# RMSNorm statistics of a two-layer trunk: the squares summed to one tile on GpSimd, the statistics placed behind the first group of products

## Chip, cores and metric

The kernel runs on one core of a Trainium2 chip. The metric is the device time of one execution in microseconds (us), the median of three runs. The core's engines are named as in the profile: PE (TensorE matmuls), DVE (VectorE), ACT (ScalarE), POOL (GpSimd), SP (SyncE, which issues most DMAs).

## What is computed

The reference is a trunk of two layers over 256 tokens of width 1024, in float32:

```python
for i in range(DEPTH):                       # DEPTH = 2
    h = h + 0.5 * swiglu(rmsnorm(h, ffn1_norm[i]), ffn1_w_up[i], ffn1_w_down[i])
    h = h + token_mixer(rmsnorm(h, mix_norm[i]), ...)   # FoX | retention | SSD | HGRN2, one W_in, one W_out
    h = h + 0.5 * swiglu(rmsnorm(h, ffn2_norm[i]), ffn2_w_up[i], ffn2_w_down[i])
    gate = sigmoid(rmsnorm(h, ple_norm[i]) @ ple_w_gate[i])
    h = h + gate * (p[i] @ ple_w_proj[i])
return rmsnorm(h, final_norm)

def rmsnorm(x, w):
    return x * lax.rsqrt(jnp.mean(x * x, axis=-1, keepdims=True) + 1e-6) * w
```

There are eight norms ahead of products (four in each layer) and a last one on the output.

## The kernel before

The state H lies transposed in SBUF: 128 partitions hold 128 of the 1024 channels, and `H[:, d]` (d = 0 to 7) is one such slice over 256 tokens. Every product is computed from float32 operands that are split in a high and a low part. `weight` brings 512 KB of a matrix to a buffer `raw`; L166 casts it on ACT to the high part `wh`, L167 subtracts on DVE for the low part `wl`. Some 360 such weights, one behind the other, are the stream that PE lives on.

**A norm.** `Norm.part` (L189) forms slice d of the normalised input without its row factor: `y` is H times the gain, high part on ACT (L194), low part on DVE (L195). The row factor 1/rms is applied to the products, afterwards. So the first products can start when the first slices of H are there, and the statistics follow: `square` (L203) squares two slices at a time on ACT (L205, 128x512); GpSimd adds the squares of slices 0 to 5 (L207, two adds of 128x512) and folds the sum to 128x256 (L210); slices 6 and 7 stay a tile of their own. `stats` (L212) sums over partitions on PE: `mm2` (L112) multiplies a 128x128 block by a column of ones in two matmuls of 64 output rows; one block of the folded tile and two of the last tile for either half of the tokens make 12 matmuls, which are 24 records in the trace. `rsqrt` (L233) makes the factors out of the two columns by nine small DVE operations (L237 to L246). `spread` (L225) copies them over the partitions by two transposing matmuls (`rows`, L106), and ACT copies that to the tile `rb` (L229), which every later scaling reads.

**Where that stands.** `col_group` (L261) and `col_tiles` emit the first group of products of a norm: four units (ffn) or two column tiles (mixer, gate) in an order in which each slice of the norm is used as it comes. `xn.scale()` (stats and rsqrt) stands at step 24 of 32 of that group, `xn.spread()` at its end. In `ffn` (L335) the group's four units are the first two of 22 gate/up pairs; `product` (L348) then adds the two halves of a bank, multiplies by the row factor (L358), applies SiLU and splits the result. Each later pair f takes two `unit`s and one `product`. In the down phase each of eight output slices is scaled, added to H, and is the next norm's part. In `mixer` the group gives hf and hq, the inputs of HGRN2 (`scaled`, L432); then come two token tiles `hv` of 264 columns (L294 to L296, in one bank of pool p and one of m), which hold also the eight small columns of dt and the forget gate (`small`, lines from L720), and after these the list PROJ. HGRN2 begins with a sigmoid and a logarithm (L571 to L577, a table load on ACT among them), a scan (L599), differences (L638 to L650), the scores (L674, L679 on PE, `qt` from L666) and masks (L690), and gives its output at L706. The last norm of layer 1 is inside `ending`, whose own call of `scale` is between products.

**What sets the order.** The program text is one order; a list scheduler decides for each engine which ready instruction is issued next, by priorities that follow the program text, and each engine runs its own list strictly in order. So text that moves lets other instructions move too. PSUM banks come from pools p (2), m (2) and a (4); squares from a pool of seven tiles m2; weights from 4 `raw`, 8 `wh` and 8 `wl`.

Of the kernel before, what the change touches and what calls it, by code (L numbers as in the profile page):

```python
# [14 lines left out]
AF = mybir.ActivationFunctionType  # L15
# [4 lines left out]
P = 128  # L20
S = 256
# [13 lines left out]
AHEAD = 2  # L35
START = "x0 u00 u10 x1 u20 u30 u01 x2 u11 u21 x3 u31"
LAG = 6
SCALE_AT = 24
ORDER = (3, 2, 1, 0)
PROJ = ("fv", "bc", "rq", "xs", "fk", "rk", "hg", "fq", "sz", "rg")  # L40

# [23 lines left out]
def trunk(ctx, tc, x, pt, par_d, con_d, w_d, ws_d, fin_d, out):  # L65
# [18 lines left out]
    def tw(kind, dt=F32, width=1024):  # L84
        if kind in ("raw", "wh", "wl"):
            return T([P, WIDE], kind, dt, NB[kind])[:, 0:width]
        return T([P, 512], kind, dt, NB[kind])
# [10 lines left out]
    def v2(t):  # L98
        return t.rearrange("p (a b) -> p a b", a=2)

    def flat(t):
        return t.rearrange("p a b -> p (a b)")
# [5 lines left out]
    def mm2(o, lhsT, rhs, start, stop):  # L108

        for u in range(2):  # L110
            r = slice(64 * u, 64 * u + 64)
            mm(o[r], lhsT[:, r], rhs, start=start, stop=stop, skip_group_check=True)  # L112
# [71 lines left out]

    class Norm:
        def __init__(self):
            self.x, self.h, self.l, self.sq = [], [], [], []

        def part(self, d, l, name, first=False):  # L189
            if d % 2 == 0:  # L190
                self.y = pair()
            y = self.y[:, d % 2]
            w = prm(l, name, d)
            A.mul(y[:, 0], H[:, d], w)  # L194
            V.scalar_tensor_tensor(y[:, 1], H[:, d], w, y[:, 0].bitcast(F32),  # L195
                                   ALU.mult, ALU.subtract)
            self.x.append(flat(y))
            self.h.append(y[:, 0])
            self.l.append(y[:, 1])
            if d % 2 and not first:  # L200
                self.square(d // 2)

        def square(self, c):  # L203
            sq = tw("m2")
            A.activation(sq, flat(H[:, 2 * c:2 * c + 2]), AF.Square)  # L205
            if self.sq and c < 3:
                G.tensor_add(sq, sq, self.sq.pop())  # L207
            self.sq.append(sq)
            if c == 2:
                G.tensor_add(sq[:, 0:S], sq[:, 0:S], sq[:, S:])  # L210

        def stats(self):  # L212
            self.b = bank("a")
            n = len(self.sq)
            for c, sq in enumerate(self.sq):
                for d in range(1 if c == 0 else 2):
                    for t in range(2):
                        mm2(self.b[:, t:t + 1], v2(sq)[:, d, t * P:(t + 1) * P], ones1,
                            c == 0 and d == 0 and t == 0, c == n - 1 and d == 1)

        def scale(self):
            self.stats()
# [38 lines left out]
    def col_group(units, xn, one, terms, arrival=None, lag=0):  # L261

        rank = arrival or (lambda u, k: k // 2)
        order = sorted((rank(u, k), u, k) for u in range(len(units)) for k in range(KD))
        for n in range(len(order) + lag):
            if n == len(order) * SCALE_AT // 32:
                xn.scale()
            if n < len(order):
                one(units[order[n][1]], order[n][2], terms[0])
            if n >= lag:  # L270
                one(units[order[n - lag][1]], order[n - lag][2], terms[1])
        xn.spread()

    def col_tiles(targets, xn, k_outer=False):
        def one(unit, k, terms=(0, 1, 2)):
# [59 lines left out]
    def ffn(xn, l, name, after_first=None, arrival=None, lag=0):  # L335
# [9 lines left out]
        def one(unit, k, terms=(0, 1)):  # L345
            b, (wh, wl) = unit
            prod2(b, wh[:, k], wl[:, k], xn.x[k], k == 0, k == KD - 1, terms)
# [19 lines left out]

        units = [unit() for _ in range(4)]
        col_group(units, xn, one, ((0,), (1,)), arrival, lag)
        for f in range(2):  # L370
            product(units[2 * f][0], units[2 * f + 1][0])
        for f in range(2, NF // P):
            units = [unit(), unit()]
            for u in units:
                for k in range(KD):
                    one(u, k)
            if f == 7 and after_first is not None:
                after_first()
            product(units[0][0], units[1][0])
# [45 lines left out]
    def mixer(l, xn):  # L425
# [26 lines left out]
        def projections():  # L452
            ba, bb = bank("p"), bank("p")
            wa, wb = by_column(), by_column()
            col_tiles(((ba, wa), (bb, wb)), xn, k_outer=True)
            got["hf"] = scaled(ba, o=v2(tw("h2")))
            got["hq"] = scaled(bb, o=keep("hq"))
            yield
            hv = keep("hv")
            bh = [bank("p"), bank("m")]  # L460
            for n, w in enumerate(by_row(2, HIW)):
                token_tiles([b[:, 0:HIW] for b in bh], w, xn, 4 * n, (n == 0, n == 0), n == 1)
                yield
            for t in range(2):
                A.mul(hv[:, t], bh[t][:, 0:256], xn.col[:, t:t + 1])
            got["hv"] = hv
# [596 lines left out]
            begin[n](int(st[2]))  # L1063
    A.dma_start(con[:, :128], con_d[:, :128])
    A.dma_start(par[1], par_d[1])
    for c in range(4):
        xn.square(c)

    def arrival(u, k):
        return max(steps.index(f"x{k // 2}"), steps.index(f"u{u}{k // 4}"))  # L1070
# [1 line left out]
    for l in range(DEPTH):  # L1072
# [13 lines left out]
        for c in range(4):  # L1086
# [5 lines left out]
                         ph[:, k], pl[:, k], m == 0 and k == 0, k == 1)  # L1092
            bp.append(b)

        def gate(c):
            w = by_column()
            z = tw("m2")
            b = bank("a")
            col_tiles(((b, w),), xn, k_outer=(c == 0))
            V.tensor_mul(v2(z), v2(b), xn.rb)  # L1100
            A.activation(z, z, AF.Sigmoid)
            V.tensor_mul(z, z, bp[c])  # L1102
            V.tensor_add(hpair(c), hpair(c), z)
# [117 lines left out]
```

## Time and profile before

| | us |
|---|---|
| median of three runs | 1112.73 |
| lowest and highest | 1109.96 and 1114.6 |
| profiled execution, its own time | 1111.85 |
| span in that profile | 1110.1 |

The profile is one execution of the program. The span is what lies between its first and last instruction; 1.75 us of the execution lie around it. Its mean granted clock of PE is 0.996. Of the page the first part gives each engine's busy time, the fourth the chain of work that ended last, followed back from the end. "Idle before" is how long an engine stood still ahead of an instruction, with an arrow to what released it. Matmuls are pipelined, so neighbours in a list overlap: what one costs is read from the distance of starts.

### The profile page before, as it was taken

What the parts mean: (1) busy time and instruction counts of PE and PEld (TensorE: products, weight loads), DVE (VectorE), ACT (ScalarE), POOL (GpSimd) and SP (SyncE); (2) the same over time, 40 slices, a digit from 0 to 9 for tenths busy, and PEclk for the clock granted to TensorE, in tenths of its full rate; (3) what the DMA queues carried; (4) which work ended last, traced back from release to release, by engine and by line L of the source; (5) the groups of instructions that cost most, each with busy time, mean ns of one, the idle gap of its engine ahead of it and who ended that gap; (6) DMA issues with size and microseconds to landing.
All of it is one profiled execution on the core that took longest, in us unless ns stands there. A gap on an engine that the chain in (4) does not pass through costs nothing.

```text
span 1110.1 us, 18572 instructions
## 1 busy us (share of the span) xinstructions
PE 1080.3 (97%) x7178; PEld 960.0 (86%) x7178; DVE 839.0 (76%) x1454; ACT 638.8 (58%) x1063; POOL 39.9 (4%) x40
## 2 busy tenths in 40 slices
PE   7999999999999999999999999999999999999996
PEld 5888888889897888888988888898899888888885
DVE  6887767599779777767878777757997787777655
ACT  6665545445477555544668555545446765555443
POOL 2000001000001000000000000001000100000001
PEclk9999999999999999999999999999999999999998
DMA  8776556135356655555555666651444476655541
GB/s 261 263 252 188 187 188 190 58 118 186 117 170 200 218 190 188 185 182 188 181 168 176 210 189 187 188 172 54 130 141 153 139 256 194 189 188 185 187 134 38
DMA packets 55432, 193.96 MB, mean 175 GB/s; under 512 B 6576, under 2 KB 7088, under 8 KB 55344
## 3 DMA queue, kind: packets, MB, share of 16 engines
q1 hardware_dynamic: 54192, 191.06, 53.8%
q10 hardware_dynamic: 1152, 1.72, 0.5%
q8 instruction: 56, 0.92, 0.3%
q14 instruction: 32, 0.26, 0.1%
HBM read 190.66 MB, written 1.05 MB: 173 GB/s over the span
## 4 chain that ended last, share of the span: by engine, by line
PE 84%; DVE 9%; ACT 3%; DMA 3%; issue 2%; SPq 0%; ACTq 0%; DVEq 0%
PE bank_a L257 27%; PE bank_a L259 14%; PE bank_p L251 10%; PE bank_m L257 8%; PE bank_p L257 8%; PE bank_m L259 4%; PE bank_p L259 4%; PE bank_a L251 3%; DVE wl L167 2%; DMA raw<-w 2%; DVE wl L690 1%; ACT wh L166 1%; DVE qt L666 1%; PE bank_a L112 1%; DVE y L195 1%
## 5 line engine op out<-in xcount | busy, mean ns | idle before, releaser
L167 DVE TENSOR_TENSOR wl<-raw,wh 128x1024 fp32r<-128x1024 f32 (+2 forms) x360 | 438.0, 1223 | 174.7 <-ACT wh L166 174.0
L166 ACT CAST wh<-raw 128x1024 fp32r<-128x1024 f32 (+2 forms) x360 | 371.7, 1040 | 328.6 <-issue 194.3
L257 PE MATMUL bank_a<-y,wh 128*128 128x512 f32 x576 | 203.0, 394 | 0.0
L259 PE MATMUL bank_a<-y,wl 128*128 128x256 f32 x576 | 161.8, 281 | 0.0
L257 PE MATMUL bank_p<-y,wh 128*128 128x512 f32 x416 | 150.6, 399 | 7.8 <-DVE y L195 7.8
L257 PE MATMUL bank_m<-y,wh 128*128 128x512 f32 x416 | 150.3, 397 | 0.2 <-DVE m L1102 0.2
L251 PE MATMUL bank_p<-y,wh 128*128 128x256 f32 x720 | 135.8, 287 | 0.0
L257 PEld LDWEIGHTS bank_a<-y,wh 128*128 128x128 f32 x576 | 108.1, 188 | 25.0
L259 PE MATMUL bank_m<-y,wl 128*128 128x256 f32 x416 | 116.1, 281 | 5.0 <-DVE wl L167 5.0
L259 PE MATMUL bank_p<-y,wl 128*128 128x256 f32 x416 | 117.1, 282 | 0.0
L251 PEld LDWEIGHTS bank_p<-y,wh 128*128 128x128 f32 x720 | 111.5, 189 | 2.7 <-issue 1.7
L259 PEld LDWEIGHTS bank_a<-y,wl 128*128 128x128 f32 x576 | 108.5, 188 | 0.0
L251 PE MATMUL bank_p<-y,wl 128*128 128x256 f32 x360 | 102.3, 284 | 0.9 <-DVE wl L167 0.9
L257 PEld LDWEIGHTS bank_p<-y,wh 128*128 128x128 f32 x416 | 78.5, 189 | 26.7 <-ACT wh L166 6.6
L257 PEld LDWEIGHTS bank_m<-y,wh 128*128 128x128 f32 x416 | 78.6, 189 | 18.6 <-issue 0.5
L259 PEld LDWEIGHTS bank_m<-y,wl 128*128 128x128 f32 x416 | 78.3, 189 | 5.8 <-DVE wl L167 5.6
L259 PEld LDWEIGHTS bank_p<-y,wl 128*128 128x128 f32 x416 | 78.6, 189 | 0.2
L251 PE MATMUL bank_a<-y,wh 128*128 128x256 f32 x384 | 71.8, 285 | 0.0
L251 PEld LDWEIGHTS bank_p<-y,wl 128*128 128x128 f32 x360 | 68.1, 189 | 1.5 <-DVE wl L167 1.0
L251 PEld LDWEIGHTS bank_a<-y,wh 128*128 128x128 f32 x384 | 59.6, 189 | 0.4 <-issue 0.3
L207 POOL TENSOR_TENSOR m<-m,m 128x512 f32<-128x512 f32 x16 | 22.0, 1374 | 959.5 <-ACT m L205 664.9
L251 PE MATMUL bank_a<-y,wl 128*128 128x256 f32 x192 | 54.0, 284 | 0.0
(419 smaller groups left out, 1897.1 us busy)
## 6 DMA issues: line engine op xcount, KB each, us to landing
raw<-w SPq DMA_DIRECT2D x348, 512.0 KB, 4.1
raw<-ws SPq DMA_DIRECT2D x4, 528.0 KB, 4.5
raw<-w SPq DMA_DIRECT2D x8, 256.0 KB, 5.1
con<-con SPq DMA_DIRECT2D x3, 512.0 KB, 7.4
H<-x SPq DMA_DIRECT2D x4, 256.0 KB, 5.8
m<-rk SPq DMA_DIRECT2D x8, 64.0 KB, 4.0
m<-rq SPq DMA_DIRECT2D x8, 64.0 KB, 2.2
m<-pt ACTq DMA_DIRECT2D x2, 256.0 KB, 3.4
```

What stands on the lines that cost most here:

```text
L112: mm(o[r], lhsT[:, r], rhs, start=start, stop=stop, skip_group_check=True)
L166: A.copy(h[:, cs], r[:, cs])
L167: last_dve[0] = V.tensor_sub(lo[:, cs], r[:, cs], h[:, cs].bitcast(F32)).ins
L195: V.scalar_tensor_tensor(y[:, 1], H[:, d], w, y[:, 0].bitcast(F32), ALU.mult, ALU.subtract)
L207: G.tensor_add(sq, sq, self.sq.pop())
L251: mm(o, wl if n == 2 else wh, xl if n == 1 else xh, start=first and n == 0, stop=last and n == 2, skip_group_check=True)
L257: mm(b, wh, x, start=first, stop=False, skip_group_check=True)
L259: mm(b[:, S:], wl, x[:, 0:S], start=False, stop=last, skip_group_check=True)
L666: V.tensor_mul(o, q0, e0)
L690: V.copy_predicated(pf[r].rearrange("p (h c n two e) -> p c h n two e", h=8, c=2, two=2, e=L)[:, u, :, :, 1], K("lvl", m, m + 32)[r].rearr ...
```

## The change

1. **Squares.** `square` is called for each slice. Slices 0 to 5 go in pairs as before, with the fold behind them. Then slice 6 and slice 7 are each squared alone (128x256) into the free half of the sum's tile and added on GpSimd (128x256). Each of the two squares has to wait for GpSimd's operation before it, which still reads that half.
2. **Statistics.** `stats` has one tile left: 4 matmuls instead of 12, so 8 records in a trace instead of 24.
3. **Place.** `col_group` calls neither `scale` nor `spread`. In `ffn` the next pair, f = 2, is emitted first: `scale` behind its first unit, `spread` behind its second, and the two products of the group after that. In `mixer` the two token tiles hv come directly behind the group, in two banks of pool m, with `scale` and `spread` behind the first and the second half; hf and hq are scaled after that. In the gate of layer 0 the products of the second slice pair are put between `scale` and `spread`. The place in `ending` stays.

```diff
--- before.py
+++ after.py
@@ -35,7 +35,6 @@
 AHEAD = 2
 START = "x0 u00 u10 x1 u20 u30 u01 x2 u11 u21 x3 u31"
 LAG = 6
-SCALE_AT = 24
 ORDER = (3, 2, 1, 0)
 PROJ = ("fv", "bc", "rq", "xs", "fk", "rk", "hg", "fq", "sz", "rg")
 
@@ -184,7 +183,7 @@
 
     class Norm:
         def __init__(self):
-            self.x, self.h, self.l, self.sq = [], [], [], []
+            self.x, self.h, self.l = [], [], []
 
         def part(self, d, l, name, first=False):
             if d % 2 == 0:
@@ -197,26 +196,29 @@
             self.x.append(flat(y))
             self.h.append(y[:, 0])
             self.l.append(y[:, 1])
-            if d % 2 and not first:
-                self.square(d // 2)
-
-        def square(self, c):
-            sq = tw("m2")
-            A.activation(sq, flat(H[:, 2 * c:2 * c + 2]), AF.Square)
-            if self.sq and c < 3:
-                G.tensor_add(sq, sq, self.sq.pop())
-            self.sq.append(sq)
-            if c == 2:
-                G.tensor_add(sq[:, 0:S], sq[:, 0:S], sq[:, S:])
+            if not first:
+                self.square(d)
+
+        def square(self, d):
+
+            if d < 6:
+                if d % 2:
+                    sq = tw("m2")
+                    A.activation(sq, flat(H[:, d - 1:d + 1]), AF.Square)
+                    if d > 1:
+                        G.tensor_add(sq, sq, self.sq)
+                    self.sq = sq
+                if d == 5:
+                    G.tensor_add(sq[:, 0:S], sq[:, 0:S], sq[:, S:])
+                return
+            sq = self.sq
+            A.activation(sq[:, S:], H[:, d], AF.Square)
+            G.tensor_add(sq[:, 0:S], sq[:, 0:S], sq[:, S:])
 
         def stats(self):
             self.b = bank("a")
-            n = len(self.sq)
-            for c, sq in enumerate(self.sq):
-                for d in range(1 if c == 0 else 2):
-                    for t in range(2):
-                        mm2(self.b[:, t:t + 1], v2(sq)[:, d, t * P:(t + 1) * P], ones1,
-                            c == 0 and d == 0 and t == 0, c == n - 1 and d == 1)
+            for t in range(2):
+                mm2(self.b[:, t:t + 1], self.sq[:, t * P:(t + 1) * P], ones1, t == 0, True)
 
         def scale(self):
             self.stats()
@@ -263,13 +265,10 @@
         rank = arrival or (lambda u, k: k // 2)
         order = sorted((rank(u, k), u, k) for u in range(len(units)) for k in range(KD))
         for n in range(len(order) + lag):
-            if n == len(order) * SCALE_AT // 32:
-                xn.scale()
             if n < len(order):
                 one(units[order[n][1]], order[n][2], terms[0])
             if n >= lag:
                 one(units[order[n - lag][1]], order[n - lag][2], terms[1])
-        xn.spread()
 
     def col_tiles(targets, xn, k_outer=False):
         def one(unit, k, terms=(0, 1, 2)):
@@ -367,13 +366,17 @@
 
         units = [unit() for _ in range(4)]
         col_group(units, xn, one, ((0,), (1,)), arrival, lag)
-        for f in range(2):
-            product(units[2 * f][0], units[2 * f + 1][0])
+        first = [(units[2 * f][0], units[2 * f + 1][0]) for f in range(2)]
         for f in range(2, NF // P):
             units = [unit(), unit()]
-            for u in units:
+            for n, u in enumerate(units):
                 for k in range(KD):
                     one(u, k)
+                if f == 2:
+                    (xn.scale, xn.spread)[n]()
+            if f == 2:
+                for pair_of in first:
+                    product(*pair_of)
             if f == 7 and after_first is not None:
                 after_first()
             product(units[0][0], units[1][0])
@@ -453,14 +456,14 @@
             ba, bb = bank("p"), bank("p")
             wa, wb = by_column(), by_column()
             col_tiles(((ba, wa), (bb, wb)), xn, k_outer=True)
+            hv = keep("hv")
+            bh = [bank("m"), bank("m")]
+            for n, w in enumerate(by_row(2, HIW)):
+                token_tiles([b[:, 0:HIW] for b in bh], w, xn, 4 * n, (n == 0, n == 0), n == 1)
+                (xn.scale, xn.spread)[n]()
             got["hf"] = scaled(ba, o=v2(tw("h2")))
             got["hq"] = scaled(bb, o=keep("hq"))
             yield
-            hv = keep("hv")
-            bh = [bank("p"), bank("m")]
-            for n, w in enumerate(by_row(2, HIW)):
-                token_tiles([b[:, 0:HIW] for b in bh], w, xn, 4 * n, (n == 0, n == 0), n == 1)
-                yield
             for t in range(2):
                 A.mul(hv[:, t], bh[t][:, 0:256], xn.col[:, t:t + 1])
             got["hv"] = hv
@@ -1063,8 +1066,8 @@
             begin[n](int(st[2]))
     A.dma_start(con[:, :128], con_d[:, :128])
     A.dma_start(par[1], par_d[1])
-    for c in range(4):
-        xn.square(c)
+    for d in range(KD):
+        xn.square(d)
 
     def arrival(u, k):
         return max(steps.index(f"x{k // 2}"), steps.index(f"u{u}{k // 4}"))
@@ -1092,12 +1095,23 @@
                          ph[:, k], pl[:, k], m == 0 and k == 0, k == 1)
             bp.append(b)
 
+        banks = {}
+
+        def products(c):
+            banks[c] = bank("a")
+            w = by_column()
+            col_tiles(((banks[c], w),), xn, k_outer=(c == 0))
+
         def gate(c):
-            w = by_column()
+            if c == 0:
+                products(0)
+                xn.scale()
+                products(1)
+                xn.spread()
+            elif c > 1:
+                products(c)
             z = tw("m2")
-            b = bank("a")
-            col_tiles(((b, w),), xn, k_outer=(c == 0))
-            V.tensor_mul(v2(z), v2(b), xn.rb)
+            V.tensor_mul(v2(z), v2(banks[c]), xn.rb)
             A.activation(z, z, AF.Sigmoid)
             V.tensor_mul(z, z, bp[c])
             V.tensor_add(hpair(c), hpair(c), z)
```

In the new text the lines are numbered anew: L166 is the subtraction for `wl` (before L167), L111 the statistics' matmul (L112), L105 the transpose (L106), L239 to L248 the rsqrt (L237 to L246), L435 `scaled` (L432), L580 the start of HGRN2 on DVE (L577), L643 its third difference (L640).

What moves is shown at two places. The first is DVE in the first ffn of layer 0, around the factors of the first norm (rv, ry and rt are the three small tiles of rsqrt, wl a weight's low part, m a product's tile). Before:

```order
L238 TENSOR_SCALAR ry_33_227<-rv_32_226 128x2
L240 SCALAR_TENSOR_TENSOR rt_34_228<-ry_33_227 128x2
L167 TENSOR_TENSOR wl_167<-raw_165,wh_166 128x1024
L241 TENSOR_TENSOR rt_34_228<-rt_34_228,rv_32_226 128x2
L242 SCALAR_TENSOR_TENSOR rt_34_228<-rt_34_228 128x2
L243 SCALAR_TENSOR_TENSOR ry_33_227<-rt_34_228,ry_33_227 128x2
L167 TENSOR_TENSOR wl_289<-raw_287,wh_288 128x1024
L244 SCALAR_TENSOR_TENSOR rt_34_228<-ry_33_227 128x2
L357 TENSOR_TENSOR m_35_264<-m_35_264,bank_p_155 128x256
L245 TENSOR_TENSOR rt_34_228<-rt_34_228,rv_32_226 128x2
L361 TENSOR_TENSOR m_35_264<-m_35_264,bank_m_156 128x256
L246 SCALAR_TENSOR_TENSOR ry_33_227<-rt_34_228,ry_33_227 128x2
```

After:

```order
L166 TENSOR_TENSOR wl_340<-raw_338,wh_339 128x1024
L243 TENSOR_TENSOR rt_41_274<-rt_41_274,rv_39_272 128x2
L166 TENSOR_TENSOR wl_347<-raw_345,wh_346 128x1024
L244 SCALAR_TENSOR_TENSOR rt_41_274<-rt_41_274 128x2
L166 TENSOR_TENSOR wl_397<-raw_395,wh_396 128x1024
L245 SCALAR_TENSOR_TENSOR ry_40_273<-rt_41_274,ry_40_273 128x2
L360 TENSOR_TENSOR m_46_326<-m_46_326,bank_a_244 128x256
L246 SCALAR_TENSOR_TENSOR rt_41_274<-ry_40_273 128x2
L166 TENSOR_TENSOR wl_404<-raw_402,wh_403 128x1024
L247 TENSOR_TENSOR rt_41_274<-rt_41_274,rv_39_272 128x2
L356 TENSOR_TENSOR m_56_383<-m_56_383,bank_a_337 128x256
L248 SCALAR_TENSOR_TENSOR ry_40_273<-rt_41_274,ry_40_273 128x2
```

Before, two subtractions stand among the nine operations; after, four, and they are the ones of the weights that follow the pair f = 2.

The second place is DVE in the mixer of layer 0, where HGRN2 starts (h, lk, hb and kk are its tiles, sm and smo those of `small`, dc a sum from PE, cc a sum from PE that `small` leads to). Before:

```order
L432 TENSOR_TENSOR hq_2149<-bank_p_1997,rb_2145 128x512
L577 SCALAR_TENSOR_TENSOR h_348_2152<-h_346_2147,h_347_2151 128x512
L720 SCALAR_TENSOR_TENSOR sm_366_2274<-bank_p_2168,ry_344_2108,par_65 128x8
L578 TENSOR_TENSOR lk_2154<-h_348_2152,h_346_2147 128x512
L599 SCALAR_TENSOR_TENSOR hb_2162<-con,h_348_2152 128x512
L720 SCALAR_TENSOR_TENSOR sm_366_2274<-bank_m_2169,ry_344_2108,par_65 128x8
L601 TENSOR_TENSOR h_349_2164<-hq_2149,kk_2153 128x512
L603 TENSOR_TENSOR lk_2154<-lk_2154,hb_2162 128x512
L617 COPY dc_2215<-bank_a_2206 128x8
L638 COPY h_362_2220<-hb_2162 128x2x64
L639 TENSOR_TENSOR h_362_2220<-hb_2162 128x2x64
L640 TENSOR_TENSOR h_362_2220<-lk_2154,hb_2162 128x2x64
```

After:

```order
L857 COPY cc_2289<-bank_m_2284 128x8
L580 SCALAR_TENSOR_TENSOR h_354_2203<-h_352_2198,h_353_2202 128x512
L581 TENSOR_TENSOR lk_2205<-h_354_2203,h_352_2198 128x512
L602 SCALAR_TENSOR_TENSOR hb_2213<-con,h_354_2203 128x512
L604 TENSOR_TENSOR h_355_2215<-hq_2200,kk_2204 128x512
L606 TENSOR_TENSOR lk_2205<-lk_2205,hb_2213 128x512
L620 COPY dc_2263<-bank_a_2254 128x8
L641 COPY h_371_2268<-hb_2213 128x2x64
L642 TENSOR_TENSOR h_371_2268<-hb_2213 128x2x64
L643 TENSOR_TENSOR h_371_2268<-lk_2205,hb_2213 128x2x64
L644 TENSOR_TENSOR h_371_2268<-lk_2205,hb_2213 128x2x64
L166 TENSOR_TENSOR wl_2296<-raw_2294,wh_2295 128x1024
```

Before, HGRN2's first operation on DVE (L577) follows `scaled` directly and the chain of `small` comes after the differences; after, all of `small` up to its last copy (cc) stands ahead of HGRN2's first operation (L580), and a weight's subtraction (wl_2296) stands behind the differences.

## Rows read from the trace of the kernel before

**Rows 1.** The page: busy time of each engine, and the chain that ended last.

```profile
PE 1080.3 (97%) x7178; PEld 960.0 (86%) x7178; DVE 839.0 (76%) x1454; ACT 638.8 (58%) x1063; POOL 39.9 (4%) x40
...
PE 84%; DVE 9%; ACT 3%; DMA 3%; issue 2%; SPq 0%; ACTq 0%; DVEq 0%
```

**Rows 2.** Windows: stretch, length, busy PE, PEld, DVE, ACT, POOL, clock, DMA share, GB/s.

```profile
220.00:240.00 20.00, 18.47 (x161) 15.25 (x160) 19.11 (x55) 10.40 (x20) 0.84 (x1) 1.00 0.34 106
...
320.00:345.00 25.00, 22.25 (x166) 20.66 (x163) 21.86 (x25) 17.01 (x25) 3.42 (x3) 1.00 0.59 190
...
765.00:785.00 20.00, 17.86 (x141) 15.03 (x140) 17.93 (x52) 10.57 (x20) 0.58 (x1) 0.91 0.33 105
```

**Rows 3.** Chain of waits, mixer of layer 0: start, length, engine, tile, line, count.

```profile
197.00 8.59 PE bank_p L251 x72
205.58 0.80 PE bank_a L112 x24
```

**Rows 4.** Timeline of GpSimd, second ffn's norm of layer 0: start, length, instruction, idle before.

```profile
335.24 2.71 POOL L207 TENSOR_TENSOR m<-m,m 128x512 f32<-128x512 f32 x2 [114.40 <-DVE y L195]
338.03 0.79 POOL L210 TENSOR_TENSOR m<-m 128x256 f32<-128x256 f32 x1
```

**Rows 5.** Timeline of DVE, first norm of layer 0.

```profile
21.23 0.15 DVE L241 TENSOR_TENSOR rt<-rt,rv 128x2 f32<-128x2 f32 x1
21.42 0.16 DVE L242 SCALAR_TENSOR_TENSOR rt<-rt 128x2 f32<-128x2 f32 x1
...
21.70 1.23 DVE L167 TENSOR_TENSOR wl<-raw,wh 128x1024 fp32r<-128x1024 f32 x1
22.84 0.15 DVE L244 SCALAR_TENSOR_TENSOR rt<-ry 128x2 f32<-128x2 f32 x1
...
23.64 0.15 DVE L246 SCALAR_TENSOR_TENSOR ry<-rt,ry 128x2 f32<-128x2 f32 x1
```

**Rows 6.** Timeline of DVE, mixer of layer 0.

```profile
210.49 0.69 DVE L432 TENSOR_TENSOR h<-bank_p,rb 128x512 f32<-128x512 f32 x1 [2.33 <-ACT rb L229]
...
214.58 0.69 DVE L577 SCALAR_TENSOR_TENSOR h<-h,h 128x512 f32<-128x512 f32 x1 [2.80 <-ACT h L576]
...
219.01 1.98 DVE L640 TENSOR_TENSOR h<-lk,hb 128x128 f32<-128x128 f32 x1
```

**Rows 7.** Timeline of ACT, mixer of layer 0.

```profile
211.96 1.28 ACT L573 ACT_TABLE_LOAD   x1
```

**Rows 8.** Timeline of PE, mixer of layer 0.

```profile
222.64 2.15 PE L674 MATMUL bank_a<-qt,kt 128*128 128x128 f32 x16 [1.36 <-DVE qt L666]
...
249.89 0.40 PE L706 MATMUL bank_a<-wl,hv 128*64 128x128 f32 x2 [0.36 <-DVE wl L690]
```

**Rows 9.** Timeline of PE, mixer of layer 1.

```profile
772.45 3.74 PE L674 MATMUL bank_a<-qt,kt 128*128 128x128 f32 x16 [2.14 <-ACT wh L166]
...
797.54 0.40 PE L706 MATMUL bank_a<-wl,hv 128*64 128x128 f32 x2 [0.36 <-DVE wl L690]
```

**Rows 10.** Windows, mixer of layer 1.

```profile
770.00:775.00 5.00, 2.86 (x13) 2.36 (x12) 4.89 (x16) 2.79 (x6) 0.00 (x0) 0.74 0.01 2
775.00:780.00 5.00, 5.00 (x44) 4.26 (x43) 3.58 (x13) 3.23 (x6) 0.00 (x0) 0.92 0.68 210
```

**Rows 11.** Timeline of DVE, second ffn's norm of layer 0.

```profile
335.74 2.50 DVE L195 SCALAR_TENSOR_TENSOR y<-H,par,y 128x256 fp32r<-128x256 f32 x2
338.16 1.75 DVE L167 TENSOR_TENSOR wl<-raw,wh 128x1024 fp32r<-128x1024 f32 x1
339.83 0.87 DVE L195 SCALAR_TENSOR_TENSOR y<-H,par,y 128x256 fp32r<-128x256 f32 x2
```

**Rows 12.** Timeline of PE, second ffn's norm of layer 0.

```profile
339.96 0.39 PE L259 MATMUL bank_m<-y,wl 128*128 128x256 f32 x1 [2.75 <-DVE wl L167]
```

**Rows 13.** Timeline of ACT, the ending.

```profile
1087.53 1.28 ACT L1033 ACT_TABLE_LOAD   x1 [3.16 <-DVE ry L246]
```

**Rows 14.** Timeline of DVE, mixer of layer 1.

```profile
758.45 0.69 DVE L577 SCALAR_TENSOR_TENSOR h<-h,h 128x512 f32<-128x512 f32 x1 [2.80 <-ACT h L576]
```

## The prediction

> **What bounds the kernel now.** I read the page first. PE is busy 97% of the span and holds 84% of the chain that ended last; DVE, at 76%, holds 9% of it [rows 1]. So time goes only with matmuls taken from PE, and comes with every new PE idle. The second view is the windows by stage: outside the first and last 25 us, PE stands still in few places, and there DVE is near full. In the mixer of layer 0, DVE works 19.1 of 20 us while PE misses 1.5; at the second ffn's norm PE misses 2.75; in the mixer of layer 1, 2.1 [rows 2]. The change moves DVE work in all three. The third view is the chain around one norm: 72 matmuls of 256 columns take 8.59 us (0.119 each, so about 0.23 for 512 columns), and directly behind them the statistics take 0.80 us for 24 records, 33 ns a record, in the same row without a gap [rows 3]. They lie on the path.
>
> **What is removed.** 16 records less per norm at 33 ns: 0.53 us, eight times, 4.3 us in all. That is 0.39% of the time, under the 0.5% (5.6 us) that a measurement here can tell from no change. The Trainium skill ("TensorE: Matmul & The Clock Gate", section on LDWEIGHTS) gives a weight load a time that grows with its columns; for the 64 columns of these matmuls an estimate by it is 53 ns a record, 6.8 us in all and a forecast 2.5 us lower. The trace has a duration, 33 ns, and it decides.
>
> **What is added.** Per norm two GpSimd adds of 128x256. One such fold took 0.79 us [rows 4]; GpSimd is 4% busy, so 16 of them fit. But a square on ACT waits for each, and the operations behind that square in ACT's list (weight casts) wait with it. ACT is 58% busy; away from a norm's start this is covered.
>
> **What moves, norm by norm** (profiled execution, 1111.85 us; it lies 0.9 below the median, and the three runs spread over 4.7, so I leave the sum where it falls).
>
> *First norm.* The nine rsqrt operations start 0.195 us apart; before, two weight subtractions stand among them, 1.14 us each from start to start, and they end at 23.64 [rows 5]. After, the statistics run one unit later, at about 24.8, and four subtractions and four small adds stand among the nine: 4 x 1.14 + 9 x 0.195 + 4 x 0.34 = 7.7 us at least, 32.8, and some 33.9 if the subtractions' casts wait for their weights as before. PE reaches the transposes five eighths into the fourth unit behind the group (2.8 us each, ending the group at 22.0): 22.0 + 0.3 + 3.6 x 2.8 = 32.4. So PE waits 1.5 us, with 0 and 3 as the ends (casts never late; each later subtraction held up once). Net +1.0.
>
> *Mixer of layer 0.* Before, hf and hq are scaled at 210.49, and HGRN2 begins on DVE at 214.58 [rows 6], behind a table load of 1.28 us on ACT [rows 7]. After, two half token tiles (24 matmuls of 264 columns, 2.9 us each) come between group and transposes, so scaling starts about 5 us later, at 215.5; the 17 small operations of `small` and a second table load now stand ahead, and HGRN2 begins at some 220.7, 6.1 us later. PE meanwhile has more to do, as the hv tiles no longer stand behind: by counting matmuls in the two orders at the rates above, 48.1 us of PE work lie between the group's end and HGRN2's output instead of 45.4. But it idles in new places: 1.3 us where the FoX value tiles want the two banks of pool p that hf and hq still hold, 1.3 at the sum that waits for the scan, and 3.8 where a weight's subtraction stands behind the third difference, the operation that took 1.98 us beside GpSimd [rows 6]. DVE paces from there on. My walk ends with HGRN2's output at 255.0 instead of 249.89 [rows 8]: 5.1 later for 2.7 more done, +2.4; with the statistics, +1.9. The ends are 0 (the idles close up) and +6.1 (the delay passes on whole, nothing covered).
>
> *The clock.* An idle of 2.14 us in the mixer of layer 1 [rows 9] was followed by a granted clock of 0.74 and 0.92 in two stretches of 5 us, that is 3.4 us at the lower of the two levels (1.2 GHz) [rows 10]; the same 16 score matmuls took 3.74 us there and 2.15 in layer 0 [rows 8, 9], where PE had idled 1.36. That is a price of 1.6 us. The new idle of 3.8 in layer 0 is longer than the one that brought it, so I add 1.6; the ends are 0 and 3.2.
>
> *The two second ffns.* Here POOL's two adds run 335.24 to 337.95, and DVE's pair of `y` beside them takes 2.50 us against 0.87 two rows later [rows 4, 11]; the next subtraction is 1.75, and PE waits 2.75 us for it [rows 12]. Two more adds now follow in that place, and the third weight's cast waits for a square that waits for POOL. The cost of that is not in the trace: between nothing and one add, 0.79. I take 0.6, as DVE is the last wait here. Net +0.1, twice.
>
> *Gate of layer 0, first ffn of layer 1, ending.* In the first two, transposes come after a column tile or two units, by which rsqrt (1.75 us) is long done: -0.5 each. In the ending, PE's statistics lead straight through rsqrt to the table load that waits for it [rows 13]: -0.5.
>
> *Mixer of layer 1.* Same move as in layer 0: HGRN2 begins at 764.4 instead of 758.45 [rows 14], its output at 801.4 instead of 797.54 [rows 9], 3.9 later, for 51.4 us of PE work instead of 46.2. The idle is cut in many pieces of under 1.8 us, so the 1.6 us of lower clock go. Net -1.25, with the statistics -1.8; ends -3.4 and +2.
>
> **The sum.** +1.0 (first norm) +1.9 +1.6 (mixer 0, clock) +0.2 (two second ffns) -1.6 (gate, ffn, ending) -1.8 (mixer 1) = +1.3: 1113.1 us. The 4.3 us are saved and given back where DVE's list got longer ahead of something PE wants.
>
> **Rivals.**
>
> *B: the saving stays.* The list scheduler's new waits close up (a reorder absorbed by the deep list of weights that is ready), mixer 0 and the first norm lose nothing, and the lower clock of mixer 1 goes: -4.3 - 1.6, 1106.0. For it: PE is 97% busy and more of its work stands ahead of HGRN2. Against: DVE had 0.9 us free in 20 [rows 2], and its list there is in strict order.
>
> *C: slower, the mixers are paced by DVE.* Place: HGRN2's start, behind `small`. If both delays, 6.1 and 6.0, reach PE whole, because the matmuls that should cover them wait too (value tiles for banks, the rest for the subtraction behind the differences), the kernel gives 12.1 for 4.3: +7.8, 1119.7. It decides from 9.9 us lost in the two mixers (4.3 + 5.6). For it: DVE is full there [rows 2]. Against: in my walk half of the delay finds other matmuls.
>
> *D: GpSimd holds DVE.* The pair of `y` that took 2.50 us instead of 0.87 beside two adds [rows 4, 11] lost 1.63 us, 0.8 per add. If each of the two new adds in the first norm and the two second ffns holds DVE for its whole 0.79 us, and PE waits for DVE there, that is 6 x 0.79 = 4.7 us; 1.2 of it is in the sum, so 1116.6. The Trainium skill ("SBUF — State Buffer", section "SBUF: two separate sides") says that a VectorE operation with two SBUF inputs and a GpSimd operation that reads SBUF lock each other out of a shared port pair for a whole instruction; the trace agrees, with 2.50 against 0.87. Against D as a whole: by the time of the new adds most of DVE's `y` is done.
>
> *E: the change does less than it says.* The removed records could have been hidden; but the chain has them directly behind matmuls [rows 3], so I give this no chance of its own.
>
> **How the numbers follow.** My forecast (with its bounds) 0.56, B 0.18, C 0.16, D 0.10. Faster by over 0.5% means below 1107.2: most of B and the lowest edge of the forecast, 0.16. Slower means above 1118.3: nearly all of C, some of D and the forecast's upper edge, 0.21. Between, 0.63. The range goes from B's time to C's, 1106.0 to 1119.7, which leaves out some 0.1 on either side; the forecast's own ends (first norm, mixer 0 and clock at their bounds) lie within it.
>
> **What would show it.** Right: eight groups of 8 records in place of 24; PE idle of 1 to 2 us at the first norm's transposes; HGRN2 in layer 0 beginning 5 to 7 us later, a PE idle of 3 to 4 us some 4 us behind that, and the lower clock after it; no lower clock in the mixer of layer 1. Wrong: no new idle in mixer 0 (B), HGRN2's outputs 6 us late in both layers with no more PE work ahead of them (C), or `y` and subtractions at twice their length beside POOL in three norms, with PE waiting for them (D).

## The result: slower, and where the time went

The changed kernel takes 1124.2 us (median of 4 runs, 1123.09 to 1125.3) against 1112.97 of the kernel before in the same comparison: ratio 1.0108, with a 95% interval of 1.0082 to 1.0134. That is slower by 11.2 us by the medians (12.0 by the ratio), outside the range that was given (1106.0 to 1119.7), and on the side that had a chance of 0.21.

The page of the changed kernel, its first part, answers to [rows 1]:

```profile
PE 1083.3 (97%) x7050; PEld 959.0 (85%) x7050; DVE 846.0 (75%) x1454; ACT 642.1 (57%) x1071; POOL 52.6 (5%) x56
```

The 128 records of the statistics are gone (7178 to 7050). But the span grew from 1110.1 to 1121.7 us: PE stands idle 38.4 us instead of 29.8, and is busy 3.0 us longer although it has less to do. The second is the sign of a lower clock, and of waits whose restart the busy time swallows.

To see where, I cut both traces at the same events: the first or last DVE operation that writes H in each part. The differences in the table are worked out from the starts of those operations in the timelines; the ending goes from the last write of H to the end of ACT's last DMA issue.

| from one write of H to another | before, us | changed, us | change | forecast |
|---|---|---|---|---|
| start to the end of ffn 1, layer 0 | 200.09 | 200.19 | +0.1 | +1.0 |
| mixer, layer 0 | 135.05 | 141.64 | +6.6 | +3.5 |
| ffn 2, layer 0, to its first output slice | 135.68 | 137.74 | +2.1 | +0.1 |
| gate of layer 0 and ffn 1 of layer 1, to its first output slice | 161.18 | 163.87 | +2.7 | -1.1 |
| mixer, layer 1 | 137.55 | 137.86 | +0.3 | -1.8 |
| ffn 2, layer 1, to its first output slice | 135.90 | 136.25 | +0.4 | +0.1 |
| ending | 35.53 | 34.67 | -0.9 | -0.5 |

The three down phases between them took 0.4 us more together.

**The mixer of layer 0.** DVE's timeline of the changed kernel, at the place of [rows 6]:

```profile
215.69 0.69 DVE L435 TENSOR_TENSOR h<-bank_p,rb 128x512 f32<-128x512 f32 x1
...
221.12 0.68 DVE L580 SCALAR_TENSOR_TENSOR h<-h,h 128x512 f32<-128x512 f32 x1
...
225.40 1.98 DVE L643 TENSOR_TENSOR h<-lk,hb 128x128 f32<-128x128 f32 x1
...
227.50 1.21 DVE L166 TENSOR_TENSOR wl<-raw,wh 128x1024 fp32r<-128x1024 f32 x1
```

Scaling comes 5.2 us later than before, HGRN2 begins 6.5 us later, and the weight's subtraction stands behind the third difference, as was read from the order. PE's timeline there:

```profile
216.52 0.47 PE L293 MATMUL bank_p<-wh,y 128*128 128x512 f32 x1 [1.42 <-DVE h L435]
...
228.77 0.80 PE L294 MATMUL bank_p<-wl,y 128*128 128x512 f32 x1 [3.84 <-DVE wl L166]
...
229.37 0.63 PE L295 MATMUL bank_p<-wh,y 128*128 128x512 f32 x1
229.79 0.63 PE L293 MATMUL bank_p<-wh,y 128*128 128x512 f32 x1
```

The wait of 1.42 us for the banks of hf and hq and the one of 3.84 us for the subtraction were forecast at 1.3 and 3.8. But behind the second the matmuls of 512 columns start 0.42 us apart, where 0.23 is usual. The windows of the changed kernel say why; the third number from the end is the granted clock, in which the lower of the two levels (1.2 and 2.4 GHz) reads 0.50:

```profile
225.00:230.00 5.00, 1.23 (x3) 1.04 (x4) 4.96 (x10) 0.83 (x2) 2.01 (x1) 0.77 0.06 8
230.00:235.00 5.00, 5.00 (x18) 4.23 (x18) 4.96 (x8) 1.85 (x3) 0.00 (x0) 0.55 0.78 245
345.00:350.00 5.00, 3.37 (x13) 2.94 (x14) 5.00 (x5) 2.77 (x5) 2.39 (x3) 0.72 0.31 105
350.00:355.00 5.00, 5.00 (x28) 4.37 (x28) 2.93 (x3) 1.78 (x2) 0.00 (x0) 0.94 0.80 270
```

PE is at the lower level for (0.23 + 0.45) x 5 / 0.5 = 6.8 us, twice what [rows 10] showed. Between the next two windows of 1 us the clock reads 0.50 throughout, so this stretch begins at 227.7 and ends at 234.5:

```profile
227.00:228.00 1.00, 0.00 (x0) 0.00 (x0) 1.00 (x3) 0.00 (x0) 0.23 (x1) 0.85 0.00 0
...
234.00:235.00 1.00, 1.00 (x5) 0.75 (x4) 0.97 (x3) 0.44 (x2) 0.00 (x0) 0.73 0.83 188
```

PE starts again only at 228.77, so 1.1 us of it lie within the idle and cost nothing more; the other 5.8 us cost half of their length, 2.9 us, where 1.6 were put in. All idle rows of this mixer together are 7.2 us, 4.3 more than before. 4.3 + 2.9 - 0.5 (the records) make 6.7, and 6.6 were measured.

**The second ffn of layer 0.** PE's wait for a subtraction is 2.86 us, as before (2.75, [rows 12]); but this time 3.4 us of the lower level follow (the last two windows above), all of it with PE at work, so 1.7 us of cost, and 0.57 us is waited at the transposes.

**The gate of layer 0.** PE waits for y three times, and once 0.21 us for a bank that DVE still reads; before, one such wait for a bank, 0.16 us, was the only idle row of the stretch:

```profile
557.36 0.47 PE L257 MATMUL bank_m<-y,wh 128*128 128x512 f32 x1 [0.16 <-DVE m L1102]
```

PE, DVE and GpSimd in the timeline of the changed kernel:

```profile
565.49 0.50 PE L259 MATMUL bank_p<-y,wh 128*128 128x512 f32 x1 [0.60 <-DVE y L194]
566.91 0.50 PE L259 MATMUL bank_p<-y,wh 128*128 128x512 f32 x1 [0.57 <-DVE y L194]
...
572.79 0.50 PE L259 MATMUL bank_p<-y,wh 128*128 128x512 f32 x1 [0.57 <-DVE y L194]
```

```profile
564.96 1.90 DVE L194 SCALAR_TENSOR_TENSOR y<-H,par,y 128x256 fp32r<-128x256 f32 x2
...
571.15 1.58 DVE L194 SCALAR_TENSOR_TENSOR y<-H,par,y 128x256 fp32r<-128x256 f32 x1
```

```profile
565.19 1.38 POOL L209 TENSOR_TENSOR m<-m,m 128x512 f32<-128x512 f32 x1 [27.41 <-ACT m L207]
571.16 1.29 POOL L209 TENSOR_TENSOR m<-m,m 128x512 f32<-128x512 f32 x1 [4.59 <-ACT m L207]
```

The gate's last update of H comes 37.7 us after the last slice of the ffn, 7.3 later than before, because the first two slice pairs wait for two column tiles and the transposes. By then the next ffn's first group has nothing else to run, and PE waits for y, which is stretched by a GpSimd add beside it in the two DVE rows shown. By the distance of starts each of those three waits costs about 0.3 us more than its idle row says.

**The statistics themselves.** In the ending, the chain of waits of the changed kernel has them at

```profile
1096.38 0.35 PE bank_a L111 x8
```

against 0.82 us for 24 records in the same place before:

```profile
1083.86 0.82 PE bank_a L112 x24
```

That is 0.47 us saved here, not 0.53. The ending is the one part that keeps it.

### The profile page after: what moved, and what is told of

Read it like the earlier page. It is cut to its first block, busy times and chain, and to the rows that moved or that the text cites. A ratio compares the mean times of both kernels' runs of the same rounds, so it can differ in the third digit from the quotient of the medians.

```text
span 1121.7 us, 18298 instructions
## 1 busy us (share of the span) xinstructions
PE 1083.3 (97%) x7050; PEld 959.0 (85%) x7050; DVE 846.0 (75%) x1454; ACT 642.1 (57%) x1071; POOL 52.6 (5%) x56
## 4 chain that ended last, share of the span: by engine, by line
PE 81%; DVE 10%; ACT 3%; DMA 3%; issue 2%; POOL 0%; SPq 0%; ACTq 0%; DVEq 0%; POOLq 0%
PE bank_a L259 26%; PE bank_a L261 13%; PE bank_p L253 9%; PE bank_m L259 8%; PE bank_p L259 8%; PE bank_m L261 4%; PE bank_p L261 4%; DVE wl L166 3%; PE bank_a L253 2%; DMA raw<-w 2%; ACT wh L165 1%; DVE wl L693 1%; DVE y L194 1%; DVE qt L669 1%; PE bank_p L294 1%
## 5 line engine op out<-in xcount | busy, mean ns | idle before, releaser
L166 DVE TENSOR_TENSOR wl<-raw,wh 128x1024 fp32r<-128x1024 f32 (+2 forms) x360 | 439.2, 1227 | 184.0 <-ACT wh L165 183.2
L261 PE MATMUL bank_a<-y,wl 128*128 128x256 f32 x576 | 162.1, 281 | 0.0
L194 DVE SCALAR_TENSOR_TENSOR y<-H,par,y 128x256 fp32r<-128x256 f32 x64 | 47.3, 757 | 10.6 <-ACT y L193 10.6
```

The lines of the kernel that those rows point to most:

```text
L166: last_dve[0] = V.tensor_sub(lo[:, cs], r[:, cs], h[:, cs].bitcast(F32)).ins
L261: mm(b[:, S:], wl, x[:, 0:S], start=False, stop=last, skip_group_check=True)
```

## The experiments

Two theories stood at the start. P: the new place of statistics and products costs, and the sums save. G: the added GpSimd adds hold DVE and delay casts.

**The sums alone.** The kernel before, with the two parts "Squares" and "Statistics" of the change and nothing else.

> The kernel before with the new sums alone: slices 6 and 7 added on GpSimd, 8 records of statistics in place of 24, every norm's statistics at their old place. Theory P (the place costs, the sums save): the 4.3 us are saved whole, about 1108.6 us. Rival G (the added GpSimd adds hold DVE and delay casts): what the change lost beyond the saving, 15.5 us, comes with the sums, so 1120 to 1124 us. Between them, 1112 to 1116, the sums give back what they save.

Measured: 1111.22 us against 1111.55, ratio 0.9994 (0.9977 to 1.0011): no difference. So the sums do not cost the 15 us that G says; nor do they save the 4.3 of P. Its timelines of PE and of GpSimd at the first norm show what takes the saving:

```profile
18.31 0.40 PE L112 MATMUL bank_a<-ones,m 128*64 128x1 f32 x8 [1.24 <-POOL m L217]
```

```profile
17.53 0.73 POOL L217 TENSOR_TENSOR m<-m 128x256 f32<-128x256 f32 x1 [0.53 <-ACT m L216]
```

The statistics now wait for the last square and the last add, and PE with them: 1.24 us here, 0.58 in the gate of layer 0, 0.21 in the ffn behind it. The rest of the difference to 3.8 us (8 x 0.47) is not in these waits, and it stays open. The execution that was profiled is no guide to it: it had no lower clock before its last 7 us and took 1106.58 us, the shortest of ten that reach up to 1114.57. Over all ten the mean granted clock, which is on record for each, runs from 0.998 down to 0.992, the longest having the lowest; but their mean, 0.9947, is that of the kernel before in the same comparison, 0.9949. So the lower clock doesn't explain the missing part either.

**The place alone.** The changed kernel with the squares and statistics of before.

> The changed kernel with the old squares and 24 records of statistics: only the place is new. Theory P: the changed kernel's 1124.2 us plus the 4.3 us not saved, about 1128 us, and the idle of 3.8 us with the lower clock behind it is still there in the mixer of layer 0. Rival G: about 1113 us, as before.

Measured: 1126.16 us (1124.42 to 1127.0), ratio 1.0129. Theory P holds. The idle of 3.84 us and the lower clock behind it (0.77 and 0.55) are there to the hundredth. With the new place the sums save 2.0 us.

**The mixer put back.** In the changed kernel:

```diff
-            col_tiles(((ba, wa), (bb, wb)), xn, k_outer=True)
-            hv = keep("hv")
-            bh = [bank("m"), bank("m")]
-            for n, w in enumerate(by_row(2, HIW)):
-                token_tiles([b[:, 0:HIW] for b in bh], w, xn, 4 * n, (n == 0, n == 0), n == 1)
-                (xn.scale, xn.spread)[n]()
+            col_tiles(((ba, wa), (bb, wb)), xn, k_outer=True, inside=True)
             got["hf"] = scaled(ba, o=v2(tw("h2")))
             got["hq"] = scaled(bb, o=keep("hq"))
             yield
+            hv = keep("hv")
+            bh = [bank("p"), bank("m")]
+            for n, w in enumerate(by_row(2, HIW)):
+                token_tiles([b[:, 0:HIW] for b in bh], w, xn, 4 * n, (n == 0, n == 0), n == 1)
+                yield
```

Here `inside=True` means statistics at step 24 of 32 of the group and transposes at its end, as before.

> The changed kernel with the mixer's projections as before (statistics inside the column group, hv behind it, banks p and m, both yields); ffn and gate keep the new place. By the traces the stretch from the first ffn's output to the mixer's last update of H grew 6.6 us in layer 0 and 0.5 in layer 1. If the mixers' order is the main part (theory P), about 1124.2 - 8 = 1116 us, with HGRN2 starting some 5 us behind the group again and no lower clock there. If the loss sits in GpSimd's adds (rival G), at most 2 us are won: 1122 or more.

Measured: 1113.77 us (1109.91 to 1118.03), ratio 1.0014 (0.9996 to 1.0033). Against the changed kernel's 1124.2 that is 10.4 us for the mixers' order. The stretch of layer 0 is back at 134.28 us, with no lower clock in it (in layer 1 the clock falls at two places).

**The gate put back**, with `inside=True` in its first column tile.

> The changed kernel with the gate of layer 0 as before (statistics inside its first column group, each slice pair finished before the next one's products). By the traces the stretch from the second ffn's output to the next ffn's down phase grew 2.8 us. Theory P: 2.8 us and the statistics' place are the cause, about 1121 us, without the PE waits for y at 565 to 573 us. Rival G: those waits stay, since the GpSimd adds of the next norm stand beside the same y operations, 1123.5 to 1124.5 us.

Measured: 1121.21 us (1120.33 to 1123.68), 3.0 less than the changed kernel; the stretch of the gate and the next ffn takes 160.61 us against 163.87. The waits for y are gone. One pair of y is still stretched to 1.91 us by GpSimd, yet nobody waits for it: the hold costs only where the order has made y late. DVE's timeline of this kernel:

```profile
558.90 1.91 DVE L194 SCALAR_TENSOR_TENSOR y<-H,par,y 128x256 fp32r<-128x256 f32 x2
```

**ffn put back**: the products of the first two pairs directly behind the group, statistics inside it.

> The changed kernel with the place in ffn as before (statistics inside the first group, products directly behind it); mixer and gate keep the new place. By the traces ffn's new place costs 0.5 us in the first norm, 2.5 in the second ffn of layer 0 (most of it lower clock behind an idle that was there before) and 0.9 in that of layer 1. Theory P: about 1120.3 us, no PE wait at the transposes. Rival G (the GpSimd adds make the idle that brings the lower clock): that idle and clock stay, only the waits at the transposes go, about 1122.5.

Measured: 1123.56 us (1122.57 to 1125.94), 0.6 less: neither value, and within the spread. The waits at the transposes go; in their place PE waits 1.24 us for GpSimd's last add at the first norm, as in the sums alone, and the second ffn of layer 0 still idles 2.88 us and falls to the lower clock. The clock also falls behind that first wait (0.50 and 0.65 from 20 to 24 us). The place in ffn hides the longer way of the sums and, by these times, costs about what it hides.

The parts make 10.4 (mixers) + 3.0 (gate) + 0.6 (ffn) - 2.0 (sums) = 12.0, against 11.2 by the medians. Each is a difference to 1124.2 us, which was measured in another comparison: there the kernel before took 1112.97 us, in these 1111.55 and 1111.68. So each part is uncertain by 1 us or more; the mixers' share stands far outside that, and the gate's is borne out by its stretch.

**Why the mixer: late factors or a new order of tiles?** The statistics go back inside the group, while the rest of the mixer stays changed:

```diff
-            col_tiles(((ba, wa), (bb, wb)), xn, k_outer=True)
+            col_tiles(((ba, wa), (bb, wb)), xn, k_outer=True, inside=True)
...
-                (xn.scale, xn.spread)[n]()
```

> The changed kernel; in the mixer alone the statistics and transposes go back inside the column group, while the token tiles hv stay directly behind it, in two banks of pool m, without the yields. The stretch from the first ffn's last H to the mixer's last H took 135.05 us before, 141.64 in the changed kernel and 134.28 with the old mixer. Theory L (the row factors come too late): 134 to 136 us, no idle of 3.8 us, no lower clock, about 1114 to 1116 us in all. Rival O (the order of the tiles, banks and yields): 139 us or more, 1121 or more in all.

Measured: 1115.29 us (1111.62 to 1116.45), stretch 135.27 us. Theory L holds. DVE's timeline of this kernel has HGRN2's start at

```profile
215.21 0.69 DVE L583 SCALAR_TENSOR_TENSOR h<-h,h 128x512 f32<-128x512 f32 x1 [2.80 <-ACT h L582]
```

and its windows the full clock where the changed kernel had 0.77 and 0.55:

```profile
225.00:230.00 5.00, 5.00 (x29) 3.87 (x28) 4.99 (x13) 1.86 (x3) 0.00 (x0) 1.00 0.77 237
230.00:235.00 5.00, 5.00 (x45) 4.09 (x44) 4.76 (x12) 4.92 (x12) 0.00 (x0) 1.00 0.49 183
```

**Is it the chain of `small` ahead of HGRN2?** In the changed kernel, `small`'s first operations are queued on DVE behind HGRN2's scan:

```diff
+        with tc.issue_after(scan):
             for t in range(2):
                 V.scalar_tensor_tensor(z[:, t], bs[t], col[:, t:t + 1], ...)
```

> The changed kernel with one order more: the first operation of the small columns is queued on DVE behind HGRN2's scan, so that HGRN2 starts ahead of that chain as it did before; factors stay late. Theory S (the chain of small operations ahead of HGRN2, some 3 us, leads to the idle of 3.8 us and the lower clock): the mixer's stretch in layer 0 falls from 141.6 to 137 or 138 us, about 1119 us in all. Theory L (the late factors alone): at most 1 us less, 1123 or more.

Measured: 1123.82 us (1122.6 to 1125.46), stretch 141.65 us: nothing won, and theory S falls: `small` ahead of HGRN2 is not what costs. HGRN2 starts only 1.4 us earlier against the ffn's end, since it waits for ACT behind the late row factors, and PE now idles ahead of the scores instead of the subtraction:

```profile
229.36 2.04 PE L677 MATMUL bank_a<-qt,kt 128*128 128x128 f32 x8 [4.29 <-DVE qt L669]
```

**What the lower clock costs.** In the changed kernel, 12 matmuls that nobody reads are put where PE stands 3.84 us:

```diff
                 at = mm(o, xh, wh[:, k], start=first[t] and k == 0, stop=False, ...)
+                if fill and t == 1 and k == 0:
+                    spare = bank("m")
+                    with tc.issue_after(at.ins):
+                        for n in range(fill):
+                            mm(spare, xh, wh[:, k], start=n == 0, stop=n == fill - 1, ...)
```

> The changed kernel with 12 more matmuls of 512 columns (2.8 us) in the mixer of layer 0, into a bank that nobody reads, placed where PE stands 3.8 us for a weight's subtraction. Nothing else waits for them. Theory C (the idle brings the lower clock, and that costs 3.4 us on top of the idle): no stretch at a granted clock under 0.99 behind it, the mixer's stretch 138 to 138.6 us instead of 141.6, about 1121 us in all, although PE does 2.8 us more work. Rival (the clock falls for another reason, or the rows after it are slow through DVE): the stretch stays at 141 us or more, 1124 in all.

Measured: 1122.72 us (1121.4 to 1124.43); stretch 140.56 us, 1.1 less with 2.8 us more work. Five of the twelve run ahead of the sum that PE awaited for 0.46 us, seven behind it. PE still waits at the end of the filling, and the lower level still comes, for half as long. From this kernel's timeline of PE and its windows:

```profile
229.12 0.50 PE L300 MATMUL bank_p<-wl,y 128*128 128x512 f32 x1 [1.47 <-DVE wl L166]
```

```profile
230.00:232.00 2.00, 2.00 (x11) 1.85 (x10) 1.97 (x3) 0.00 (x0) 0.00 (x0) 0.61 0.83 262
232.00:234.00 2.00, 2.00 (x6) 1.54 (x6) 2.00 (x4) 1.60 (x3) 0.00 (x0) 0.54 0.69 258
```

That is (0.39 + 0.46) x 2 / 0.5 = 3.4 us at the lower level instead of 6.8. All of it lies where PE works, so it costs 1.7 us instead of 2.9; the 1.2 us less are what the stretch shows (1.1), as the filling only takes the place of idle time. The idle is a cause of the lower clock, but filling most of it was not enough to keep the clock: the theory is half borne out. The medians (1122.7 and 1124.2) point the same way, but the ranges overlap.

**The idle that was there before.** If two adds of GpSimd stretch y from 0.87 to 2.50 us in the second ffn [rows 4, 11], the kernel before should gain without them (`apart` is set for the norms of the two second ffns):

```diff
+            if self.apart:
+                sq = tw("m2")
+                A.activation(sq, flat(H[:, 2 * c:2 * c + 2]), AF.Square)
+                self.sq.append(sq)
+                return
```

> The kernel before, without any GpSimd add in the two second ffns' norms: their four tiles of squares go to PE one by one, 64 records in place of 24, 1.3 us more PE time each. Theory G (GpSimd's adds hold DVE there): the pair of y that took 2.50 us takes 0.9, the PE idles of 2.75 and 2.25 us behind it shrink to under 0.5, net 2 to 2.5 us faster than before, about 1109 us. Rival (PE waits there for the weights' casts in any case): the idles stay and the time is 1113.5 to 1114.5 us.

Measured: 1108.92 us (1107.92 to 1111.48) against 1111.68, ratio 0.9979 (0.9967 to 0.9990). Theory G holds at this place. DVE and PE in its timeline, where [rows 11, 12] had 2.50, 1.75 and a wait of 2.75:

```profile
335.78 0.88 DVE L196 SCALAR_TENSOR_TENSOR y<-H,par,y 128x256 fp32r<-128x256 f32 x2
336.57 1.22 DVE L167 TENSOR_TENSOR wl<-raw,wh 128x1024 fp32r<-128x1024 f32 x1
```

```profile
337.84 0.38 PE L265 MATMUL bank_m<-y,wl 128*128 128x256 f32 x1 [0.74 <-DVE wl L167]
```

**The best of both.** To this kernel the new sums are added in the two mixers' norms and the last one, with every statistic at its old place.

> The kernel before, every statistic at its old place: the two second ffns' norms without GpSimd adds (64 records), the two mixers' norms and the last one with the new sums (8 records), the other three as before. From the stages: 2.4 us from the second ffns and 0.5 to 0.8 each from the other three, less lower clock in the mixer of layer 1 where it falls away: about 1107 us, 0.4% faster than before. If GpSimd's sums are awaited in those three as they were in three others (0.2 to 1.2 us), about 1109.

Measured: 1110.02 us (1108.09 to 1113.27) against 1112.17, ratio 0.9986 (0.9975 to 0.9997). It beats the kernel before by its interval, though by less than 0.5%, and it is not better than the one above. The stretch of mixer 0 is the shortest of all (133.40 us) and the ending keeps its saving (34.71 us), but in the profiled execution the clock falls in layer 1 at two places. Over all executions the mean granted clock is 0.9933 against 0.9953 of the kernel above; by that, an estimated 2.2 us of 1108 go back to the lower clock. One of the two places has no idle ahead of it, only the 64 records of the second ffn's statistics:

```profile
885.80 2.03 PE L112 MATMUL bank_a<-ones,m 128*64 128x1 f32 x64
```

```profile
888.00:890.00 2.00, 2.00 (x10) 1.71 (x10) 1.55 (x10) 1.29 (x3) 0.00 (x0) 0.79 0.98 383
890.00:892.00 2.00, 2.00 (x9) 1.71 (x8) 1.67 (x3) 1.24 (x3) 0.00 (x0) 0.50 0.13 53
```

## Why the prediction was wrong

- **The removed records** were right in kind: 0.47 us per norm against 0.53. What the term left out is that the sum of all eight squares is ready later than the old two tiles. At the old place three norms wait for it up to 1.24 us.
- **Mixer of layer 0** was put at +3.5 with the clock and came at +6.6. The mechanism was right (banks, late HGRN2, a subtraction behind the difference, the lower clock after the long idle); two of the three idles came to 0.1 us, the one at the sum was 0.46 instead of 1.3. Two terms were too small. The walk booked +2.4, though its own three idles, 6.4 us, stand against 2.85 us of idle rows in the same stretch before; the idle rows grew by 4.3. The clock was priced at 1.6 us from an idle of 2.1; behind 3.8 it cost 2.9. Its reason, that the new idle is longer than the one that brought the lower clock, was weak: the same trace has an idle of 2.75 us without it [rows 2, 12]. The parts of HGRN2's delay were right: scaling is 5.2 us later (forecast 5), and `small` adds 1.4 (forecast 1.1). But that last part costs nothing, since the time stays without it, and with early factors alone the stretch is 135.3. The rival C named DVE's delay as what decides; its price for layer 0 (6.1) was near the measured 6.6 partly by luck, as 2.9 of the 6.6 are lower clock, which C did not count; that for layer 1 (6.0) was not near.
- **Mixer of layer 1** was put at -1.8 and came at +0.3. In the profiled execution the lower clock went away there, as forecast, and no idle is longer than 1.6 us. The step that failed is the sum of the idles: their rows make 6.1 us against 4.4 before, 1.8 more, where the forecast left about 0.35. With the same mixer the clock still falls there in the runs of ffn put back and of `small` behind.
- **Second ffn of layer 0** was put at +0.1 and came at +2.1: no lower clock was put behind an idle that had none before, and 1.7 us of it came. That idle was followed by the lower clock in five kernels with the new mixer (2.61 to 2.88 us), and not in the kernel before (2.75) nor where it was shorter (2.02 to 2.45); why it differs at 2.75 is open. Putting both mixers back won 10.4 us, more than the two mixers' stretches show (6.6 + 0.3), so part of what is booked on this ffn hangs on the mixer ahead of it.
- **Gate of layer 0**: "transposes come after a column tile or two units, by which rsqrt (1.75 us) is long done: -0.5 each" looked at the transposes alone. The step that failed is what stands behind them: four updates of H, each the input of the next ffn's first group. They came 7.3 to 9.6 us later in the stretch, and it cost 2.7 us instead of winning 1.1.
- **Rival B** (the new waits close up) is out: PE stands idle 8.6 us longer. **Rival D** (GpSimd holds DVE) was right as a mechanism, as the kernel without those adds shows, but wrong as a price of this change: the holds that cost are those of before, and in the gate they cost only because y had become late. **First norm**: a stall of 0.67 us instead of 1.5, as forecast in kind. **Ending**: right in kind, -0.9 for -0.5.

So the forecast of +1.3 missed by 3.8 us in the gate and the ffn behind it, 3.1 in the mixer of layer 0, 2.1 in that of layer 1 and 2.0 in the second ffn of layer 0. The gate was valued by what PE does at the moved step, and not by who waits for the factors next; in the mixers the new idles were booked too small, and the lower clock behind idles was put at too little in one place and at nothing in another.

## What to carry to other kernels

A statistic that is moved later is paid by its last consumer: follow the row factors to the next operation that PE waits for, not to the transposes. Where PE is 97% busy, one new idle of some us can cost twice, once itself and once at the lower clock behind it. Here an idle avoided (GpSimd's adds taken away beside DVE, for 1.2 us more PE work each) was worth more than records saved: 2.8 us against 0.3.

## What the runs showed of the hardware that was not expected

- The lower level lasted 3.4 us behind some idles and 6.8 behind the one of 3.84 us, in four kernels alike (0.77 to 0.82, then 0.50 to 0.55 in two windows of 5 us); with 2.4 us of that idle filled it lasted 3.4. In the changed kernel the 6.8 us began within the idle, 1.1 us before PE started again.
- The same idle can come with or without it: 2.75 us without (kernel before), 2.86, 2.61 and 2.88 us with it, at the second ffn of layer 0; in layer 1 at that place 2.88 us without it (ffn put back) and 2.04 us with it (filled kernel). Ahead of the score matmuls of layer 1, 2.14 us came with it in the kernel before and 2.15 without it in the one without GpSimd adds.
- 64 records of one column in a row, 2.03 us in which PE counts as busy, were followed by the lower level in one kernel (0.79 and 0.50) and not in another that has the same 64.
